# Seven products instead of eight for more row pairs of the MLP's up projection, with part of the preparation on GpSimd

## The chip, the cores and the metric

One core of one Trainium2 chip runs the kernel. The metric is the device time of one launch in microseconds (us); the time before is the median of three runs, and one further execution was recorded by the hardware profiler. Engines are called as the profile calls them: PE (TensorE), PEld (its weight loads), DVE (VectorE), ACT (ScalarE), POOL (GpSimd) and SP (SyncE, which issues most DMAs).

## What is computed

Two layers on 256 tokens of width 2048, all in float32. Layer 0 has a convolution module, layer 1 a latent attention; each is followed by the same kind of MLP, and the change touches only the two MLPs:

```python
def sq_relu_mlp(h, w1, w2):
    return jnp.square(jax.nn.relu(h @ w1)) @ w2

for layer in range(DEPTH):
    h = rms_norm(x, norm_mixer_g[layer])
    x = x + mixer(h)                       # conv_module or mla
    h = rms_norm(x, norm_mlp_g[layer])
    x = x + sq_relu_mlp(h, mlp_w1[layer], mlp_w2[layer])
```

Here `w1` is 2048 x 8192 and `w2` is 8192 x 2048.

## The kernel before

**Three products for one.** A float32 matrix is split into an upper part `hi` (rounded by ACT to the short float32 form that PE multiplies in one pass) and a lower part `lo` (what is left: a subtraction `raw - hi`). A product is then made of three matmuls, hi x hi, lo x hi and hi x lo (`mm3`, L209 to L211). Weights arrive by DMA in tiles `raw` of 128 x 2048 numbers (three buffers), ACT writes `hi`, DVE writes `lo`; there are six buffers of 128 x 1024 for each. So every weight passes ACT and DVE before PE can use it, and these engines run ahead of PE as far as the buffers allow.

**The MLP.** It is worked in two halves of 4096 hidden columns (`hf` 0 and 1). A half has an up projection, which makes eight groups of 512 hidden columns, and then a down projection, which adds the half's share to `x` in two pairs of 512-column blocks (`Sums`, L563; the very last pair of the program in two steps). `UP_PLAN` (L47) lists the order of the up projection. Four groups are made one at a time with the weights standing in PE and the input moving (L797 to L814). The other four are made as two *blocks* of two groups each (`up_block`, L732): here the input stands in PE and 512 columns of weights move at a time. Before, the plan is group 4, group 5, block 0 and 1, group 6, block 2 and 3, group 7.

**Eight products and seven.** In a block and in the down projection, the contraction is worked in *row pairs*: two stretches of 128 rows, for two sets of 128 tokens and two sets of 512 columns. That is a product of 2 x 2 matrices whose elements are blocks: eight products of three matmuls each (`Sums.plain`, L592: 24 matmuls). `Sums.mixed` (L579) does it with seven products (21 matmuls), by sums and differences of weight blocks on one side (`mixed_weights`, L517) and of input blocks on the other (`mixed_sums`, L539). The weights of such a pair need more work ahead of PE: four tiles of hi and lo instead of two (`b11` with `b21`; `b22`, half as large; `t1` with `t3`; `t4` with `t2`), and three subtractions on `raw` in place between them (L532 to L534). These depend on each other: `t1`, `t3` come from the first subtraction, `t4`, `t2` from the last. PE takes the products in the order b11, b21, b22, t1, t3, t4, t2 (L588).

A block has eight row pairs, in the order `UP_ORDER`; those in `UP_MIXED` go by seven products, before four of eight (2, 3, 4 and 5). Their input forms are made once in a half by `up_forms` (L680): a sum of hi and lo, four sums and differences, and a split, all three kinds on DVE, with the upper parts and copies on ACT. They stand in the buffers `s`. For the plain pairs of a block a copy of the input is made (`UP_COPIES`, `up_copies`). In the down projection seven or eight of the sixteen row pairs of a pair of column blocks go by seven products, mixed among plain ones; their input forms are made by `mixed_inputs` (L546) right after a group's squared ReLU.

**What sets the order.** The MLP's instructions are put in order by the framework's scheduler when the program is built, and each engine then runs its own list strictly in that order; an instruction that waits holds up all behind it on its engine. Buffers are handed out in rotation. GpSimd has little in the MLPs: it issues the DMAs that add finished sums to `x` (L611). It works in the convolution, where it makes lower parts of weights (L180 with `nc.gpsimd`), and in the attention, where it rotates keys and queries (L1529 to L1534).

Of the kernel before, what the change touches and what calls it, by code (L numbers as in the profile page):

```python
# [10 lines left out]
F32 = mybir.dt.float32  # L11
# [32 lines left out]
MIXED = {(layer, half): tuple(range(7 + (layer + half < 2))) for layer in range(2) for half in range(2)}  # L44
N_MIXED = 4
HEAD, TAIL = (2, 1), 2
UP_PLAN, UP_ORDER, UP_MIXED = (4, 5, 0, 6, 2, 7), (0, 2, 1, 3, 6, 4, 5, 7), (2, 3, 4, 5)  # L47
UP_FORMS = ({(1, 1): 0, (1, 3): 1}, {(0, 2): 0, (1, 1): 1})
UP_COPIES = ({(1, 0): 0, (1, 2): 3}, {(1, 0): 0, (1, 2): 3})


SIDE = {KC - 3: 2, KC - 2: 4}
# [30 lines left out]
def trunk_kernel(  # L83
# [59 lines left out]
    def nm(s):  # L143
        uid[0] += 1
        return f"{s}_{uid[0]}"
# [371 lines left out]
    def mixed_weights(raw):  # L517

        def halves(src):
            hi = wpool.tile(list(src.shape), F32R, tag="hi", name=nm("hi"), bufs=WB)
            lo = wpool.tile(list(src.shape), F32R, tag="lo", name=nm("lo"), bufs=WB)
            nc.scalar.activation(hi, src, AF.Copy)  # L524
            nc.vector.tensor_tensor(lo, src, hi.bitcast(F32), op=ALU.subtract)  # L525
# [6 lines left out]
        nc.vector.tensor_tensor(top, raw[:, :, NB:], top, op=ALU.subtract)  # L532
        nc.vector.tensor_tensor(low[:, 1, :], low[:, 1, :], top[:, 0, :], op=ALU.subtract)
        nc.vector.tensor_tensor(low[:, 0, :], low[:, 0, :], low[:, 1, :], op=ALU.subtract)  # L534
        t1, t3 = halves(top)
        t4, t2 = halves(low)
        return b11, b21, b22, t1, t2, t3, t4

    def mixed_sums(a11, a21, a12, a22):  # L539

        nc.vector.tensor_tensor(a22, a21, a22, op=ALU.add)
        nc.vector.tensor_tensor(a21, a11, a21, op=ALU.subtract)
        nc.vector.tensor_tensor(a11, a22, a11, op=ALU.subtract)
        nc.vector.tensor_tensor(a12, a12, a11, op=ALU.subtract)

    def mixed_inputs(v, fh, fl):  # L546

        def halves(src, at, n):  # L550
            hi, lo = fh[:, :, at : at + n, :], fl[:, :, at : at + n, :]
            nc.scalar.activation(hi, src, AF.Copy)
            nc.vector.tensor_tensor(lo, src, hi.bitcast(F32), op=ALU.subtract)
# [98 lines left out]
    def mlp(layer, ssq, next_gain, finish=None, before=None, beside=None, after_up=None):  # L652

        with ExitStack() as cx:
# [77 lines left out]
            def up_block(hf, g, fs, copies):  # L732

                n = (hf * nkh + 4 * g) // 4
                sums = Sums(n, False, True)
                left = [p for p in UP_ORDER if p in UP_MIXED]

                def at_kt(c):
                    def at(k, t):
                        ts = slice(t * P, (t + 1) * P)  # L740
                        return copies[k // 4][c][:, k % 4, ts] if k // 4 in copies else (xh, xl)[c](k)[:, ts]
                    return at

                for p in UP_ORDER:
                    if p in UP_MIXED:
                        left.remove(p)
                        sums.mixed(mlp_w1[layer], 2 * p, up_form(p, fs), not left)
                        continue
                    end = p == UP_ORDER[-1]
                    if end:  # L750
                        zs = [v_tile().rearrange("p k n -> p (k n)") for _ in range(T)]
                        sums.parts(*(z[:, c * NB : (c + 1) * NB] for z in zs for c in range(2)))
                    sums.plain(mlp_w1[layer], 2 * p, at_kt(0), at_kt(1), 2 * p, end)
                for t, z in enumerate(zs):
                    o = z.rearrange("p (c n) -> p c n", c=2)
                    nc.vector.tensor_tensor(o, sums.pairs[t], o, op=ALU.add)
                    nc.scalar.activation(z, z, AF.Relu, scale=r_cols[0][:, t : t + 1])

                def turned():
                    pts = [a.rearrange("p b (k t n) -> p (b k) t n", t=T, n=P) for a in sums.pairs]  # L760
                    for c in range(2):
                        for f in range(4):
                            for t in range(T):
                                at = c * NB + f * P
                                nc.tensor.transpose(pts[c][:, f, t, :], zs[t][:, at : at + P], ident)  # L765
                    for c in range(2):
                        place(g + c)
                        v = v_tile()
                        nc.scalar.activation(v, pts[c].rearrange("p f t n -> p f (t n)"), AF.Square)
                        activations(g + c, v)  # L770

                return [turned]

            r_cols, late = [], []
            for hf in range(HALVES):
# [5 lines left out]
                fs = [[mp.tile([P, 2, 7, P], F32R, tag=f"s{c}", name=nm(f"f{c}"), bufs=N_MIXED) for _ in range(2)] for c in "hl"]  # L781
                copied = {
                    n: [mp.tile([P, 4, S], F32R, tag=f"g{c}", name=nm(f"x{c}"), bufs=ng - N_MIXED) for c in "hl"]
                    for n in UP_COPIES[hf].values()
                }
                for nth, g in enumerate(UP_PLAN):
# [1303 lines left out]
```

## Time and profile before

| | |
|---|---|
| median of 3 runs | 1923.65 us (1923.41 to 1924.89) |
| the profiled execution | 1923.38 us, of which the span of the records is 1921.6 us |
| granted TensorE clock over the span | 0.999 |
| PE busy | 1909.4 us (99%) |
| DVE busy | 1696.6 us (88%) |
| ACT busy | 1201.3 us (63%) |
| POOL busy | 248.6 us (13%) |
| moved by DMA | 375.43 MB |

The convolution ends and layer 0's MLP begins at 301 us, the attention follows at about 977 us, and layer 1's MLP runs from about 1237 us to the end. A row of a timeline gives the start (us from the span's start), how long, the engine, the line, the operation, what is written from what, and the shape. Matmuls overlap: a matmul of 512 columns is shown as 0.39 us long, but the next starts before it ends, so PE's pace is read from start to start. In rows of the view that groups instructions, the numbers behind the bar are the group's busy time in us and the mean of one in ns.

### The profile page before, as it was taken

The page shows a single profiled execution, that of the slowest core. Times are in us where ns is not written, and L with a number is a line of the kernel's source. Part 1 is how long each engine was busy: PE and PEld are TensorE (multiplying, and loading weights), DVE is VectorE, ACT ScalarE, POOL GpSimd, SP SyncE. Part 2 cuts the span into 40 slices and gives each one's busy share as a digit, 9 for nine tenths or more (in the row PEclk, how much of TensorE's full clock was granted, in tenths as well). Part 3 has the DMA queues.
Part 4 walks back from the last instruction along what each step waited for, and adds up shares of the span by engine and source line. Part 5 has one row for each costly group of instructions (what it writes and reads, how often), then busy time and mean ns, then how long its engine had stood idle before and what let it go on. Part 6 is the DMA issues. An engine that isn't in the chain of part 4 may idle for free.

```text
span 1921.6 us, 27587 instructions
## 1 busy us (share of the span) xinstructions
PE 1909.4 (99%) x10245; PEld 1653.2 (86%) x10245; DVE 1696.6 (88%) x2407; ACT 1201.3 (63%) x1701; POOL 248.6 (13%) x208
## 2 busy tenths in 40 slices
PE   9999999999999999999999999999999999999998
PEld 9999888888888888888888998888888888888887
DVE  7999989999999899999976765898999988898898
ACT  5667756666655666665576665576665647666554
POOL 6999200000010100000001420000000010000000
PEclk9999999999999999999999999999999999999999
DMA  7766455556585855655656445556556775655774
GB/s 228 211 185 186 156 186 196 187 186 219 176 250 198 252 167 193 229 178 199 217 168 183 138 137 177 173 176 219 188 173 225 219 246 199 219 180 195 233 221 147
DMA packets 214039, 375.43 MB, mean 195 GB/s; under 512 B 16392, under 2 KB 107792, under 8 KB 213648
## 3 DMA queue, kind: packets, MB, share of 16 engines
q1 hardware_dynamic: 208256, 363.28, 57.4%
q0 software_dynamic: 4320, 7.87, 2.2%
q10 hardware_dynamic: 1328, 2.52, 0.4%
q8 instruction: 80, 1.31, 0.3%
q14 instruction: 55, 0.45, 0.1%
HBM read 363.68 MB, written 2.10 MB: 190 GB/s over the span
## 4 chain that ended last, share of the span: by engine, by line
PE 96%; DVE 2%; ACT 1%; issue 0%; DMA 0%; DVEq 0%; ACTq 0%
PE acc L209 11%; PE acc L211 11%; PE acc L210 11%; PE pair L211 10%; PE pair L210 10%; PE pair L209 10%; PE acc L812 9%; PE acc L972 8%; PE acc L813 5%; PE pair L812 3%; PE acc L1436 2%; PE pair L813 2%; DVE sum L1059 1%; PE pair L765 1%; PE acc L1713 0%
## 5 line engine op out<-in xcount | busy, mean ns | idle before, releaser
L176 ACT ACTIVATE hi<-raw 128x1024 fp32r<-128x1024 f32 (+2 forms) x510 | 509.9, 1030 | 149.1 <-DMA raw<-in_mlp_w 44.1
L180 DVE TENSOR_TENSOR lo<-raw,hi 128x1024 fp32r<-128x1024 f32 (+2 forms) x445 | 519.2, 1193 | 89.4 <-ACT hi L176 84.7
L524 ACT ACTIVATE hi<-raw 128x1024 fp32r<-128x1024 f32 x376 | 347.0, 948 | 316.0 <-DVE raw L532 199.1
L525 DVE TENSOR_TENSOR lo<-raw,hi 128x1024 fp32r<-128x1024 f32 x376 | 400.2, 1088 | 26.9 <-ACT hi L524 21.0
L812 PE MATMUL acc<-xt,hi 128*128 128x512 f32 x768 | 268.0, 391 | 0.0
L813 PE MATMUL acc<-xt,lo 128*128 128x256 f32 x768 | 216.5, 282 | 0.0
L972 PE MATMUL acc<-xt,hi 128*128 128x256 f32 x1024 | 180.2, 281 | 0.4 <-ACT xt L1239 0.3
L611 POOL DMA_DIRECT2D xs<-v x30 | 26.3, 932 | 1128.3 <-DVE lo L180 696.2
L812 PEld LDWEIGHTS acc<-xt,hi 128*128 128x128 f32 x768 | 144.2, 188 | 30.1
L1059 DVE SCALAR_TENSOR_TENSOR sum<-ub,w_dw,sum 128x256 f32<-128x256 f32 x409 | 164.4, 485 | 3.6 <-ACT sum L1029 3.0
L180 POOL TENSOR_TENSOR lo<-raw,hi 128x1024 fp32r<-128x1024 f32 x65 | 155.0, 2408 | 18.0 <-ACT hi L176 18.0
L972 PEld LDWEIGHTS acc<-xt,hi 128*128 128x128 f32 x1024 | 154.7, 188 | 1.2 <-ACT xt L1239 0.8
L813 PEld LDWEIGHTS acc<-xt,lo 128*128 128x128 f32 x768 | 145.1, 189 | 0.3
L972 PE MATMUL acc<-xt,lo 128*128 128x256 f32 x512 | 139.2, 279 | 0.0
L532 DVE TENSOR_TENSOR raw<-raw 128x1024 f32<-128x1024 f32 x94 | 114.8, 1221 | 0.4
L209 PE MATMUL acc<-hi,sh 128*128 128x512 f32 x289 | 112.6, 390 | 0.0
L211 PE MATMUL acc<-lo,sh 128*128 128x512 f32 x289 | 112.5, 389 | 0.0
L210 PE MATMUL pair<-hi,gl 128*128 128x512 f32 (+1 forms) x264 | 101.9, 386 | 0.0
L211 PE MATMUL pair<-lo,gh 128*128 128x512 f32 (+1 forms) x264 | 101.9, 386 | 0.0
L209 PE MATMUL pair<-hi,gh 128*128 128x512 f32 (+1 forms) x264 | 101.9, 386 | 0.0
L209 PE MATMUL acc<-hi,gh 128*128 128x512 f32 x252 | 98.1, 389 | 0.0
L211 PE MATMUL acc<-lo,gh 128*128 128x512 f32 x252 | 98.0, 389 | 0.0
(381 smaller groups left out, 4299.1 us busy)
## 6 DMA issues: line engine op xcount, KB each, us to landing
raw<-in_mlp_w SPq DMA_DIRECT2D x255, 1024.0 KB, 5.5
raw<-in_conv_w_pw SPq DMA_DIRECT2D x62, 512.0 KB, 5.1
raw<-in_conv_w_pw SPq DMA_DIRECT2D x16, 1024.0 KB, 4.9
raw<-in_mla_w_o SPq DMA_DIRECT2D x16, 1024.0 KB, 5.1
raw<-in_mla_w_kv_up SPq DMA_DIRECT2D x32, 256.0 KB, 4.0
xs<-v POOLq DMA_DIRECT2D x30, 256.0 KB, 7.3
raw<-in_mla_w_in SPq DMA_DIRECT2D x8, 576.0 KB, 4.3
raw<-in_mla_w_in SPq DMA_DIRECT2D x4, 1024.0 KB
```

Of the source, the lines that this page charges most:

```text
L176: nc.scalar.activation(hi, raw[:, js, :], AF.Copy)
L180: eng.tensor_tensor(lo, raw, hi.bitcast(F32), op=ALU.subtract)
L209: nc.tensor.matmul(ps, sh, mh, start=start, stop=False)
L210: nc.tensor.matmul(ps, sl, mh, start=False, stop=False)
L211: nc.tensor.matmul(ps, sh, ml, start=False, stop=stop)
L524: nc.scalar.activation(hi, src, AF.Copy)
L525: nc.vector.tensor_tensor(lo, src, hi.bitcast(F32), op=ALU.subtract)
L532: nc.vector.tensor_tensor(top, raw[:, :, NB:], top, op=ALU.subtract)
L812: nc.tensor.matmul(ps[b], wh[:, bs], xhl(k), start=k == 0, stop=False)
L813: nc.tensor.matmul(ps[b][:, :S], wl[:, bs], xh(k), start=False, stop=k == KC - 1)
L972: nc.tensor.matmul(pss[c][b][:, :S], w[i][:, bs], (xh, xl)[j](k), start=k == i + j == 0, stop=end and k == k0 + nk - 1 and (i, j) == terms ...
L1059: nc.vector.scalar_tensor_tensor(out=out, in0=ubs[c][:, w : w + S], scalar=tap(c, w), in1=base, op0=ALU.mult, op1=ALU.add)
```

## The change

More row pairs of the blocks go by seven products: six of eight (`UP_MIXED` is 0 to 5), in the order 6, 0, 1, 2, 3, 4, 5, 7, so that the six stand side by side. The plan of the up projection becomes group 4, group 5, block 6 and 7, group 0, block 1 and 2, group 3 (`UP_BLOCKS` says which places of the plan are blocks, since a block may now consist of groups that the down projection takes by eight products). Three input forms are made instead of two, and one input tile is copied instead of two; form tiles and copies share the buffers `s`. And some work moves from DVE to GpSimd: the lower parts of `b22` and of `t1` with `t3` in every mixed row pair, the blocks' and the down projection's; everything that `up_forms` does on DVE; and the last lower part of `mixed_inputs`. What is computed is the same.

```diff
-UP_PLAN, UP_ORDER, UP_MIXED = (4, 5, 0, 6, 2, 7), (0, 2, 1, 3, 6, 4, 5, 7), (2, 3, 4, 5)
-UP_FORMS = ({(1, 1): 0, (1, 3): 1}, {(0, 2): 0, (1, 1): 1})
-UP_COPIES = ({(1, 0): 0, (1, 2): 3}, {(1, 0): 0, (1, 2): 3})
+UP_PLAN, UP_BLOCKS, UP_ORDER, UP_MIXED = (4, 5, 6, 0, 1, 3), (2, 4), (6, 0, 1, 2, 3, 4, 5, 7), (0, 1, 2, 3, 4, 5)
+UP_FORMS = ({(1, 0): 0, (1, 1): 1, (1, 2): 2}, {(0, 2): 0, (1, 0): 1, (1, 1): 2})
+UP_COPIES = ({(1, 0): 3}, {(1, 0): 3})
...
-        def halves(src):
+        def halves(src, eng=nc.vector):
...
-            nc.vector.tensor_tensor(lo, src, hi.bitcast(F32), op=ALU.subtract)
+            eng.tensor_tensor(lo, src, hi.bitcast(F32), op=ALU.subtract)
...
-        (b22,) = halves(raw[:, 1:2, NB:])
+        (b22,) = halves(raw[:, 1:2, NB:], nc.gpsimd)
...
         nc.vector.tensor_tensor(top, raw[:, :, NB:], top, op=ALU.subtract)
+        t1, t3 = halves(top, nc.gpsimd)
         nc.vector.tensor_tensor(low[:, 1, :], low[:, 1, :], top[:, 0, :], op=ALU.subtract)
         nc.vector.tensor_tensor(low[:, 0, :], low[:, 0, :], low[:, 1, :], op=ALU.subtract)
-        t1, t3 = halves(top)
         t4, t2 = halves(low)
...
-    def mixed_sums(a11, a21, a12, a22):
+    def mixed_sums(eng, a11, a21, a12, a22):
...
-        mixed_sums(*(v[:, :, i, :] for i in range(4)))
-        halves(v, 3, 4)
+        mixed_sums(nc.vector, *(v[:, :, i, :] for i in range(4)))
+        halves(v, 3, 4, nc.gpsimd)
...
-                nc.vector.tensor_tensor(v, x[:, :, :S], x[:, :, S:], op=ALU.add)
+                nc.gpsimd.tensor_tensor(v, x[:, :, :S], x[:, :, S:], op=ALU.add)
...
-                mixed_sums(*(v[:, :, j, :] for j in range(4)))
+                mixed_sums(nc.gpsimd, *(v[:, :, j, :] for j in range(4)))
...
-                nc.vector.tensor_tensor(l, v, h.bitcast(F32), op=ALU.subtract)
+                nc.gpsimd.tensor_tensor(l, v, h.bitcast(F32), op=ALU.subtract)
...
-                    if g in mixed:
-                        late = up_block(hf, g, fs, {n: a for n, a in copied.items() if nth < 3 or n > 0})
+                    if nth in UP_BLOCKS:
+                        late = up_block(hf, g, fs, copied if nth == UP_BLOCKS[0] else {})
```

PE's list has 10198 matmuls before and 10150 after, 48 fewer: three for each of two more row pairs in eight blocks.

**DVE in a block.** Before, in the second block of layer 0's first half, these are DVE's rows for the last two mixed row pairs, which stand next to each other (`raw_666` and `raw_675`; numbers behind names tell tiles apart):

```order
L525 TENSOR_TENSOR lo_668_4995<-raw_666_4992,hi_667_4994 128x1024
L525 TENSOR_TENSOR lo_670_4999<-raw_666_4992,hi_669_4998 128x512
L532 TENSOR_TENSOR raw_666_4992<-raw_666_4992 128x1024
L533 TENSOR_TENSOR raw_666_4992<-raw_666_4992 128x512
L534 TENSOR_TENSOR raw_666_4992<-raw_666_4992 128x512
L525 TENSOR_TENSOR lo_672_5006<-raw_666_4992,hi_671_5005 128x1024
L525 TENSOR_TENSOR lo_674_5010<-raw_666_4992,hi_673_5009 128x1024
L525 TENSOR_TENSOR lo_677_5037<-raw_675_5034,hi_676_5036 128x1024
```

After, at the same block, the third and fourth of the six mixed row pairs (`raw_665` and `raw_674`; the lines have moved by one, so that L534 and L535 are what L533 and L534 were):

```order
L525 TENSOR_TENSOR lo_667_4945<-raw_665_4942,hi_666_4944 128x1024
L532 TENSOR_TENSOR raw_665_4942<-raw_665_4942 128x1024
L534 TENSOR_TENSOR raw_665_4942<-raw_665_4942 128x512
L535 TENSOR_TENSOR raw_665_4942<-raw_665_4942 128x512
L525 TENSOR_TENSOR lo_673_4960<-raw_665_4942,hi_672_4959 128x1024
L525 TENSOR_TENSOR lo_676_4987<-raw_674_4984,hi_675_4986 128x1024
```

Seven rows for one row pair have become five; nothing stands any more between the last subtraction (L534 before, L535 after) and the lower part that is made of its result.

**GpSimd there.** Before, its list has only the DMAs of L611 in this MLP; after, these rows stand there for the same two row pairs and the one ahead of them (`sl_634` is the last lower part of group 0's input forms):

```order
L525 TENSOR_TENSOR lo_660_4907<-raw_656_4900,hi_659_4906 128x512
L525 TENSOR_TENSOR lo_662_4912<-raw_656_4900,hi_661_4911 128x1024
L553 TENSOR_TENSOR sl_634_4796<-v_635_4797,sh_633_4795 128x2x512
L525 TENSOR_TENSOR lo_669_4949<-raw_665_4942,hi_668_4948 128x512
L525 TENSOR_TENSOR lo_671_4954<-raw_665_4942,hi_670_4953 128x1024
L525 TENSOR_TENSOR lo_678_4991<-raw_674_4984,hi_677_4990 128x512
```

Two rows for each row pair, and one for a form, have come to GpSimd's list.

**ACT ahead of the first block.** Before, in the same half, ACT's rows around the upper part of the second (last) input form, `fh_463` (`hi_524` and `hi_537` are upper parts of weights of group 5 and of the block's first, plain row pair):

```order
L176 ACTIVATE hi_524_4182<-raw_521_4176 128x1024
L691 ACTIVATE fh_463_3801<-xt_3_98 128x2x128
L692 ACTIVATE fh_463_3801<-xt_3_98 128x2x256
L687 ACTIVATE fh_463_3801<-v_526_4218 128x2x512
L691 ACTIVATE fl_465_3803<-xt_3_98 128x2x128
L692 ACTIVATE fl_465_3803<-xt_3_98 128x2x256
L176 ACTIVATE hi_537_4253<-raw_536_4251 128x1024
```

After, around that of the third (last) form, `fh_466`:

```order
L692 ACTIVATE fl_469_3807<-xt_3_98 128x2x256
L176 ACTIVATE hi_524_4200<-raw_523_4198 128x1024
L687 ACTIVATE fh_466_3804<-v_522_4186 128x2x512
L176 ACTIVATE hi_526_4204<-raw_523_4198 128x1024
L176 ACTIVATE hi_538_4263<-raw_537_4261 128x1024
```

The form's upper part now stands ahead of group 5's last weights (`hi_526`), and it waits for GpSimd's sums.

More of the change, by code (lines that the diff above doesn't have):

```diff
@@ L532, in mixed_weights, with halves @@
         nc.vector.tensor_tensor(top, raw[:, :, NB:], top, op=ALU.subtract)
+        t1, t3 = halves(top, nc.gpsimd)
         nc.vector.tensor_tensor(low[:, 1, :], low[:, 1, :], top[:, 0, :], op=ALU.subtract)
         nc.vector.tensor_tensor(low[:, 0, :], low[:, 0, :], low[:, 1, :], op=ALU.subtract)
-        t1, t3 = halves(top)
         t4, t2 = halves(low)
         return b11, b21, b22, t1, t2, t3, t4
-    def mixed_sums(a11, a21, a12, a22):
[L541 to L544, printed above, removed]
+    def mixed_sums(eng, a11, a21, a12, a22):
+        eng.tensor_tensor(a22, a21, a22, op=ALU.add)
+        eng.tensor_tensor(a21, a11, a21, op=ALU.subtract)
+        eng.tensor_tensor(a11, a22, a11, op=ALU.subtract)
+        eng.tensor_tensor(a12, a12, a11, op=ALU.subtract)
     def mixed_inputs(v, fh, fl):
-        def halves(src, at, n):
+        def halves(src, at, n, eng=nc.vector):
             hi, lo = fh[:, :, at : at + n, :], fl[:, :, at : at + n, :]
             nc.scalar.activation(hi, src, AF.Copy)
-            nc.vector.tensor_tensor(lo, src, hi.bitcast(F32), op=ALU.subtract)
+            eng.tensor_tensor(lo, src, hi.bitcast(F32), op=ALU.subtract)
         halves(v[:, :, 0:1, :], 0, 1)
         halves(v[:, :, 2:4, :], 1, 2)
-        mixed_sums(*(v[:, :, i, :] for i in range(4)))
-        halves(v, 3, 4)
+        mixed_sums(nc.vector, *(v[:, :, i, :] for i in range(4)))
+        halves(v, 3, 4, nc.gpsimd)
     def by_pairs(v):
@@ L780, in mlp @@
                 gs = {}
-                fs = [[mp.tile([P, 2, 7, P], F32R, tag=f"s{c}", name=nm(f"f{c}"), bufs=N_MIXED) for _ in range(2)] for c in "hl"]
                 copied = {
-                    n: [mp.tile([P, 4, S], F32R, tag=f"g{c}", name=nm(f"x{c}"), bufs=ng - N_MIXED) for c in "hl"]
+                    n: [mp.tile([P, 4, S], F32R, tag=f"s{c}", name=nm(f"x{c}"), bufs=N_MIXED) for c in "hl"]
                     for n in UP_COPIES[hf].values()
                 }
+                fs = [
+                    [mp.tile([P, 2, 7, P], F32R, tag=f"s{c}", name=nm(f"f{c}"), bufs=N_MIXED) for _ in range(len(UP_MIXED) // 2)]
+                    for c in "hl"
+                ]
                 for nth, g in enumerate(UP_PLAN):
-                    if g in mixed:
-                        late = up_block(hf, g, fs, {n: a for n, a in copied.items() if nth < 3 or n > 0})
+                    if nth in UP_BLOCKS:
+                        late = up_block(hf, g, fs, copied if nth == UP_BLOCKS[0] else {})
                         continue
```

## Prediction

> **What bounds the kernel now.** First the page's busy times and its chain that ended last, then the waits of PE:
>
> ```profile
> PE 1909.4 (99%) x10245; PEld 1653.2 (86%) x10245; DVE 1696.6 (88%) x2407; ACT 1201.3 (63%) x1701; POOL 248.6 (13%) x208
> ...
> PE 96%; DVE 2%; ACT 1%; issue 0%; DMA 0%; DVEq 0%; ACTq 0%
> ```
> ```profile
> PE acc L1150 <- POOL ident masks.py:199: 1.6, 1, 1.6
> PE acc L209 <- DVE xt L222: 1.2, 1, 1.2
> ```
>
> PE bounds it: it waits 1.6 us once and 1.2 us once, and never for weights in an MLP. So matmuls left out are gained in full as long as the weights still come in time. What one is worth is read from start to start; PE's timeline over a mixed row pair of a block, from its first matmul over the second to the first of what follows:
>
> ```profile
> 441.24 0.39 PE L209 MATMUL acc<-hi,fh 128*128 128x512 f32 x1
> 441.46 0.39 PE L210 MATMUL acc<-hi,fl 128*128 128x512 f32 x1
> ...
> 446.00 0.39 PE L209 MATMUL pair<-hi,xh 128*128 128x512 f32 x1
> ```
>
> The 21 matmuls take 446.00 - 441.24 = 4.76 us, 0.2267 us each, not the 0.39 us of a record. A plain row pair's 24 take 5.44 us.
>
> The other side of a block is the preparation. The grouped view, each shape by itself:
>
> ```profile
> L525 DVE TENSOR_TENSOR lo<-raw,hi 128x1024 fp32r<-128x1024 f32 x282 | 341.7, 1222 | 26.9 <-ACT hi L524 21.0
> L532 DVE TENSOR_TENSOR raw<-raw 128x1024 f32<-128x1024 f32 x94 | 114.8, 1221 | 0.4
> L533 DVE TENSOR_TENSOR raw<-raw 128x512 f32<-128x512 f32 x94 | 65.1, 692 | 3.0
> L534 DVE TENSOR_TENSOR raw<-raw 128x512 f32<-128x512 f32 x94 | 65.0, 692 | 2.6
> L525 DVE TENSOR_TENSOR lo<-raw,hi 128x512 fp32r<-128x512 f32 x94 | 64.5, 686 | 0.0
> L524 ACT ACTIVATE hi<-raw 128x1024 fp32r<-128x1024 f32 x282 | 295.4, 1057 | 296.4 <-DVE raw L532 199.1 <-DVE raw L534 40.4 <-PE pair L210 13.8
> ```
>
> DVE needs 3 x 1.22 + 1.22 + 2 x 0.69 + 0.69 = 6.95 us for a mixed row pair that PE finishes in 4.76, and 2 x 1.22 = 2.4 us for a plain one that PE takes 5.44 us for. A mixed pair overdraws the lead, a plain one pays back. How large the lead is when a block's mixed pairs begin: DVE's first lower part for the first one, and PE's first matmul on it:
>
> ```profile
> 340.92 1.22 DVE L525 TENSOR_TENSOR lo<-raw,hi 128x1024 fp32r<-128x1024 f32 x1
> ```
> ```profile
> 351.00 0.39 PE L209 MATMUL acc<-hi,fh 128*128 128x512 f32 x1
> ```
>
> 10.1 us; the rotation of six buffers lets it hardly grow.
>
> **What goes.** 48 matmuls of 0.2267 us: 10.9 us off PE, if it never waits. On paper DVE is relieved too: 6.95 - 1.22 - 0.69 = 5.04 us per mixed pair, nearly PE's 4.76.
>
> **What the mixed pair costs now.** Two things speak against those 5.04 us. The first is a gap. ACT and DVE around the last subtractions of a pair:
>
> ```profile
> 440.18 1.06 ACT L524 ACTIVATE hi<-raw 128x1024 fp32r<-128x1024 f32 x1 [2.78 <-DVE raw L532]
> 441.63 1.06 ACT L524 ACTIVATE hi<-raw 128x1024 fp32r<-128x1024 f32 x1 [0.39 <-DVE raw L534]
> ```
> ```profile
> 440.82 0.69 DVE L534 TENSOR_TENSOR raw<-raw 128x512 f32<-128x512 f32 x1
> 441.43 2.51 DVE L525 TENSOR_TENSOR lo<-raw,hi 128x1024 fp32r<-128x1024 f32 x2
> ```
>
> The last subtraction ends at 441.51; ACT rounds its result from 441.63 to 442.69; only then can DVE make that lower part. Before, DVE fills the time with the other lower part. After, its list has nothing in between, and the next pair's rows stand behind: 1.2 us idle, 6.2 us per pair.
>
> The second is GpSimd beside DVE. GpSimd's own prices, from the views by line and by shape:
>
> ```profile
> L180 POOL TENSOR_TENSOR lo<-raw,hi x65: 2352/2409/2445, 12.7 to 197.9; 128x1024 fp32r<-128x1024 f32 x65
> ```
> ```profile
> L1748 POOL TENSOR_TENSOR qhl<-qp,qhl 128x256 fp32r<-128x256 f32 x8 | 5.8, 734 | 0.9 <-ACT qhl L215 0.9
> ```
>
> (2409 - 734) / 768 = 2.18 ns per element, so 2.41 us for 1024 columns and an estimate of 1.29 us for 512. The 2409 hold beside a DVE that in the convolution reads one operand from PSUM. In an MLP both operands of lower parts and subtractions lie in SBUF. The only place of the trace where DVE does such work while GpSimd subtracts or adds is the attention; GpSimd's timeline, then DVE's, and last DVE's two lower parts in the MLP with GpSimd idle:
>
> ```profile
> 1045.71 0.45 POOL L1531 TENSOR_TENSOR m<-scratch,cos 128x128 f32<-128x128 f32 x1
> 1046.13 1.44 POOL L1532 TENSOR_TENSOR m<-scratch,sin 128x128 f32<-128x128 f32 x1
> ...
> 1086.60 0.46 POOL L1532 TENSOR_TENSOR m<-scratch,sin 128x128 f32<-128x128 f32 x1
> 1087.02 1.49 POOL L1533 TENSOR_TENSOR qp<-m,m 128x128 f32<-128x128 f32 x1
> ```
> ```profile
> 1045.71 2.94 DVE L180 TENSOR_TENSOR lo<-raw,hi 128x1024 fp32r<-128x1024 f32 x2 [1.71 <-ACT hi L176]
> ...
> 1086.96 1.23 DVE L180 TENSOR_TENSOR lo<-raw,hi 128x1024 fp32r<-128x1024 f32 x1 [0.32 <-ACT hi L176]
> ```
> ```profile
> 444.15 2.36 DVE L180 TENSOR_TENSOR lo<-raw,hi 128x1024 fp32r<-128x1024 f32 x2 [0.20 <-PE acc L211]
> ```
>
> A GpSimd operation of 0.46 us takes 1.49 us when a DVE lower part has begun 0.06 us earlier: it ends 0.32 us after that one. And DVE loses in turn: the two lower parts from 1045.71 take 2.94 us instead of 2.36, with the two GpSimd operations of 1045.71 and 1046.13 fitted in, 0.29 us each, which is 128 x 2.18 ns. The two engines take turns. GpSimd thus costs DVE 1024 x 2.18 = 2.2 us and 512 x 2.18 = 1.1 us for a mixed pair: 5.04 + 2.2 + 1.1 = 8.3 us, with the gap hidden under GpSimd's turn. ACT's four upper parts, at most 4 x 1.06 us, stay below that, and the DMAs carry what they did before.
>
> The Trainium skill says in "SBUF — State Buffer", section "Who interferes with whom", that a VectorE instruction with two SBUF inputs contends with a GpSimd instruction that reads SBUF, and that the pair of ports is held exclusively for the whole instruction. By its whole instruction DVE would lose 2.41 + 1.29 = 3.7 us, 8.7 us per pair, and the sum below would be 35 us more; the attention's rows show turns, but only 0.29 us of a 0.46 us operation. I take the row.
>
> Ends for the hold: nothing (6.2 us per pair, as the convolution's rows would have it) and the whole operation (5.04 + 2.41 + 1.29 = 8.7 us). The attention's rows are the same operations on the same operands, so 8.3.
>
> **A block.** Six pairs stand side by side, so PE wants them in 6 x 4.76 = 28.6 us. Preparation begins 10.1 us ahead and takes six times C, and with it the evacuation of the group before, which DVE's list has among the first pairs; that and other work of the blocks:
>
> ```profile
> L832 DVE SCALAR_TENSOR_TENSOR v<-v,r_row 128x1024 f32<-128x1024 f32 x16 | 19.6, 1224 | 0.1
> L715 DVE TENSOR_TENSOR gl<-v,gh 128x1024 fp32r<-128x1024 f32 x16 | 19.5, 1221 | 2.1 <-ACT gh L714 2.1
> L541 DVE TENSOR_TENSOR v<-v 128x256 f32<-128x256 f32 x23 | 9.6, 419 | 0.1
> L553 DVE TENSOR_TENSOR sl<-v,sh 128x512 fp32r<-128x512 f32 x16 | 11.0, 689 | 0.8
> L1486 DVE SCALAR_TENSOR_TENSOR v<-v 128x64 f32<-128x64 f32 x19 | 4.3, 225 | 0.3
> ```
>
> That is 2.4 us (L832, L715). GpSimd's long lower part is ready about 1.1 us before a pair's preparation ends, and PE, which meets it as the twelfth matmul, then needs 2.3 us to end the pair: +1.2. PE's wait in a block is 6 C - 10.1 + 2.4 + 1.2 - 28.6 = 6 C - 35.1: 14.7 us for 8.3, 2.1 for 6.2, 17.1 for 8.7, none below 5.85. Eight blocks: 118 us.
>
> More is in some. The second block of a half follows group 0, which has mixed input forms: four sums of 0.42, lower parts of 0.69 and (256 columns like L541) 0.42 and GpSimd's 2.2 us, 5 us, four times: 20. In layer 0's second half some 28 small operations of the rotary tables (0.225 us, L1486) fall into the end of group 5 and the first block: 5 of their 6 us. In the first halves three forms go one behind the other through GpSimd, each 2 x 2.41 + 4 x 0.73 + ACT's 1.06 = 8.8 us, the last two behind group 4's evacuation; group 5, during which they must end, lasts from the first to the second of these rows:
>
> ```profile
> 323.36 0.39 PE L812 MATMUL acc<-xt,hi 128*128 128x512 f32 x1
> ...
> 345.54 0.39 PE L209 MATMUL pair<-hi,xh 128*128 128x512 f32 x1
> ```
>
> 17.6 of 22.2 us, and the third form's upper part stands on ACT ahead of the last eighth of group 5's weights, which PE wants 2.8 us before that end, and of all the block's. Estimate: 10 us of wait and lost lead, between 0 and 14, twice: 20. Blocks in all 163 us.
>
> **The down projection.** Eight pairs of column blocks, each about eight mixed and eight plain row pairs: 8 x (8.3 + 2.4) = 85.6 us of preparation against 8 x (4.76 + 5.44) = 81.6 of PE, 4 us more even if leads carried over everything. Where two mixed pairs and a plain one follow each other, 19.0 stand against 15.0, three times in the first pair of columns: 12. I take 8, 64 us in all (32 to 96). Fewer input sums on DVE, copies and group order change nothing that PE waits for: group 3's forms come last and are used last.
>
> **Sum**, on the profiled execution's 1923.4 us (its span and 1.8 us around; the median of the runs is 0.3 us above): - 10.9 + 163 + 64 = + 216, **2140 us**.
>
> **Rivals.**
> - *The turns don't matter at this size, only the gap does* (6.2): for it, the convolution's 2409; against, the attention's rows. Blocks 8 x 2.1 + 45, columns none (14.8 against 15.0): + 62 - 10.9, 1975 us. Chance 0.08.
> - *All is hidden, faster*: GpSimd's work falls into DVE's gaps and the lead bears the rest; decides below 5.85 us per pair. For it, DVE's 5.04; against, both rows above. 1912.5 us. Chance 0.05.
> - *PE's clock falls in the waits*: with 8.3 us per pair PE stands still for 3.5 us each time. At half the clock a pair would take 9.5 us and bound itself: 48 x 1.2 = 58 us more, 2198 us. The trace grants full speed, but has no such wait. Chance 0.05. (The Trainium skill, "TensorE: Matmul & The Clock Gate", Part 1, halves the clock after an idle window of about 3.4 us; no run here shows it.)
>
> The forecast has 0.82. With a hold of two thirds (C 7.2: blocks 8 x 8.1 + 20, no columns) it would be 1997; with the whole hold, 14 us twice and 12 per columns, 2198. Range 1990 to 2210, with which the gap alone and the gain stay out. Faster by over 0.2% (about what can be told from no change) 0.05, within 0.01, slower 0.94.
>
> **What would show it.** In the profile after, PE waits for POOL `lo` L525, and DVE's records of L525 and L532 grow past 1.22 us or POOL's past 2.41, in blocks and in the down projection; from one mixed pair's first lower part to the next 8.3 us; a block's matmuls last some 39.4 + 14.7 = 54 us instead of 4 x (4.76 + 5.44) = 41. Wrong is the turn if POOL shows 2.41 and DVE 1.22 side by side; wrong is all of it if PE has no wait in the blocks.

## The result and the profile after

The changed kernel takes 2223.9 us (median of four runs, 2221.7 to 2224.1) against 1923.6 before: 1.156 times as long, with an interval of 1.1537 to 1.1577. The forecast was 2140 us with a range up to 2210. The direction and, in the blocks' row pairs, the mechanism were right; the size was 84 us too small, 51 of them in the down projections. The profiled execution took 2223.85 us, its span is 2222.1 us.

The page's busy times:

```profile
PE 2027.1 (91%) x10197; PEld 1678.5 (76%) x10197; DVE 1806.2 (81%) x2203; ACT 1227.7 (55%) x1745; POOL 893.6 (40%) x516
```

PE has 48 matmuls less in its list, yet it is busy for 118 us more, and DVE, which was to be relieved, for 110 us more. Then the waits of PE (us in all, how often, the longest):

```profile
PE acc L211 <- POOL lo L525: 67.4, 45, 2.0
PE pair L211 <- POOL lo L525: 33.8, 20, 2.6
PE acc L209 <- ACT hi L524: 19.6, 23, 1.7
PE acc L815 <- ACT hi L176: 11.7, 6, 3.4
```

PE waited for nothing in an MLP before. Now it waits 101 us for GpSimd's lower parts (the first two rows) and another 31 us for upper parts, which are late because DVE's subtractions are (L524) or because ACT is held up (L176). The grouped view of DVE and GpSimd says what made them late:

```profile
L525 DVE TENSOR_TENSOR lo<-raw,hi 128x1024 fp32r<-128x1024 f32 x220 | 408.3, 1873 | 130.8 <-ACT hi L524 128.0 <-PE acc L210 1.2 <-PE pair L211 1.2
L532 DVE TENSOR_TENSOR raw<-raw 128x1024 f32<-128x1024 f32 x110 | 174.8, 1589 | 3.5
```
```profile
L525 POOL TENSOR_TENSOR lo<-raw,hi 128x1024 fp32r<-128x1024 f32 x110 | 277.8, 2525 | 302.8 <-ACT hi L524 187.7 <-PE pair L211 50.0 <-issue 42.5
L525 POOL TENSOR_TENSOR lo<-raw,hi 128x512 fp32r<-128x512 f32 x110 | 207.9, 1890 | 334.0 <-ACT hi L524 295.9 <-PE acc L211 17.7 <-PE pair L210 13.2
...
L553 POOL TENSOR_TENSOR sl<-v,sh 128x512 fp32r<-128x512 f32 x1 | 1.3, 1273 | 6.1 <-ACT sh L552 6.1
```

DVE's lower part was 1222 ns and its long subtraction 1221; they are 1873 and 1589. GpSimd's short lower part was estimated at 1.29 us, and the one of 512 columns outside the row pairs (L553) took 1.27; in the row pairs it shows 1.89. And in front of these lower parts of DVE stands idle time that ACT ends, once in a mixed pair: 128 us in all, about 1.2 us for each of the 110 pairs.

Where in the program this falls, from the windows view of layer 0's first half; columns: the window, its length, the busy time of PE, PEld, DVE, ACT and POOL, the granted clock, the DMA share and GB/s. The rows are groups 4 and 5, the first block, the second block, the down projection; first before:

```profile
300.92:345.54 44.62, 44.62 (x259) 39.55 (x258) 41.39 (x64) 33.13 (x48) 0.00 (x0) 1.00 0.52 177
345.54:386.36 40.82, 40.82 (x183) 33.79 (x182) 37.65 (x41) 26.30 (x32) 0.00 (x0) 1.00 0.55 189
410.31:451.44 41.13, 41.13 (x183) 33.80 (x182) 39.65 (x44) 26.78 (x33) 0.00 (x0) 1.00 0.53 181
475.40:638.62 163.22, 163.22 (x723) 135.19 (x722) 152.25 (x161) 94.32 (x108) 8.31 (x10) 1.00 0.67 212
```
```profile
300.70:355.20 54.50, 47.90 (x259) 41.31 (x258) 36.64 (x48) 32.35 (x47) 21.81 (x14) 0.94 0.38 128
355.20:414.36 59.16, 47.23 (x179) 33.90 (x178) 49.05 (x43) 31.01 (x38) 23.64 (x11) 0.94 0.39 134
437.85:498.34 60.49, 47.87 (x178) 34.99 (x177) 49.83 (x45) 30.41 (x37) 25.93 (x12) 0.92 0.35 117
521.84:713.74 191.90, 176.12 (x722) 138.20 (x721) 160.64 (x133) 95.47 (x111) 87.65 (x45) 0.96 0.56 180
```

The granted clock is a second new thing: 1.00 in each of these stages before, 0.92 to 0.96 now. Summed over the four halves, from the start of PE's first matmul in each stage, and beside it what the prediction had for the same stages (118 + 20 + 5 - 10.9 = 132 for the blocks):

| stage, four halves | before | after | forecast | measured |
|---|---|---|---|---|
| groups 4 and 5 | 178.0 | 216.2 | +20 | +38 |
| the eight blocks | 327.9 | 479.1 | +132 | +151 |
| the other two groups | 191.7 | 188.0 | 0 | -4 |
| down projections | 651.8 | 767.1 | +64 | +115 |

Last a steady stretch of a block, the fourth and fifth of the six mixed pairs; DVE's timeline, then GpSimd's:

```profile
379.30 4.33 DVE L525 TENSOR_TENSOR lo<-raw,hi 128x1024 fp32r<-128x1024 f32 x2 [1.21 <-ACT hi L524]
383.66 1.23 DVE L532 TENSOR_TENSOR raw<-raw 128x1024 f32<-128x1024 f32 x1
384.99 0.69 DVE L534 TENSOR_TENSOR raw<-raw 128x512 f32<-128x512 f32 x1
385.72 0.69 DVE L535 TENSOR_TENSOR raw<-raw 128x512 f32<-128x512 f32 x1
387.62 4.31 DVE L525 TENSOR_TENSOR lo<-raw,hi 128x1024 fp32r<-128x1024 f32 x2 [1.21 <-ACT hi L524]
391.96 1.23 DVE L532 TENSOR_TENSOR raw<-raw 128x1024 f32<-128x1024 f32 x1
```
```profile
377.81 2.51 POOL L525 TENSOR_TENSOR lo<-raw,hi 128x1024 fp32r<-128x1024 f32 x1 [2.31 <-ACT hi L524]
380.87 1.68 POOL L525 TENSOR_TENSOR lo<-raw,hi 128x512 fp32r<-128x512 f32 x1 [0.55 <-ACT hi L524]
```

From L532 to L532 a pair takes 391.96 - 383.66 = 8.30 us; 8.3 was forecast. It is made up of 5.14 us of DVE's own work, the gap of 1.21 us, and 4.31 - 2.36 = 1.95 us by which the two lower parts are longer. The gap before the lower parts at 379.30 lasts from 378.09 to 379.30 and lies wholly within GpSimd's long instruction, 377.81 to 380.32. The ends of the records show how DVE loses them. GpSimd's second instruction ends at 380.87 + 1.68 = 382.55 and DVE's second lower part at 379.30 + 4.33 = 383.63, 1.08 us later; alone that lower part needs 1.22. So all but 0.14 us of its work came behind the end of GpSimd's instruction.

### The profile page after: what moved, and what is told of

Same layout as the page of the kernel before. It is cut to its first block, busy times and chain, and to the rows that moved or that the text cites. A ratio compares the mean times of both kernels' runs of the same rounds, so it can differ in the third digit from the quotient of the medians.

```text
span 2222.1 us, 27868 instructions
## 1 busy us (share of the span) xinstructions
PE 2027.1 (91%) x10197; PEld 1678.5 (76%) x10197; DVE 1806.2 (81%) x2203; ACT 1227.7 (55%) x1745; POOL 893.6 (40%) x516
## 5 line engine op out<-in xcount | busy, mean ns | idle before, releaser
L525 POOL TENSOR_TENSOR lo<-raw,hi 128x512 fp32r<-128x512 f32 x220 | 485.3, 2208 | 636.8 <-ACT hi L524 483.6
L524 ACT ACTIVATE hi<-raw 128x1024 fp32r<-128x1024 f32 (+1 forms) x440 | 402.8, 946 | 501.5 <-DVE raw L532 329.3
L180 DVE TENSOR_TENSOR lo<-raw,hi 128x1024 fp32r<-128x1024 f32 (+2 forms) x413 | 502.5, 1247 | 137.6 <-ACT hi L176 131.5
L176 ACT ACTIVATE hi<-raw 128x1024 fp32r<-128x1024 f32 (+2 forms) x478 | 472.6, 1027 | 148.0 <-DMA raw<-in_mlp_w 69.9
L525 DVE TENSOR_TENSOR lo<-raw,hi 128x1024 fp32r<-128x1024 f32 x220 | 408.3, 1873 | 130.8 <-ACT hi L524 128.0
L532 DVE TENSOR_TENSOR raw<-raw 128x1024 f32<-128x1024 f32 x110 | 174.8, 1589 | 3.5
L211 PE MATMUL acc<-lo,fh 128*128 128x512 f32 x192 | 87.3, 470 | 57.2 <-POOL lo L525 53.6
L534 DVE TENSOR_TENSOR raw<-raw 128x512 f32<-128x512 f32 x110 | 104.3, 948 | 35.2 <-POOL lo L525 25.1
L211 PE MATMUL pair<-lo,sh 128*128 128x512 f32 x225 | 96.2, 427 | 26.2 <-POOL lo L525 23.1
L553 POOL TENSOR_TENSOR sl<-v,sh 128x1024 fp32r<-128x1024 f32 (+1 forms) x16 | 48.5, 3043 | 166.9 <-ACT sh L552 166.9
L209 PE MATMUL pair<-hi,sh 128*128 128x512 f32 x225 | 93.7, 417 | 17.1 <-ACT v L647 6.6
```

The lines of the kernel that those rows point to most:

```text
L176: nc.scalar.activation(hi, raw[:, js, :], AF.Copy)
L180: eng.tensor_tensor(lo, raw, hi.bitcast(F32), op=ALU.subtract)
L209: nc.tensor.matmul(ps, sh, mh, start=start, stop=False)
L211: nc.tensor.matmul(ps, sh, ml, start=False, stop=stop)
L525: eng.tensor_tensor(lo, src, hi.bitcast(F32), op=ALU.subtract)
```

## The experiments

All times are medians; "changed" is the changed kernel, 2223.9 us. Lines in these kernels can lie up to five off those of the changed one; `...` in a diff stands for lines left out.

**1. All on DVE.** GpSimd's new work goes back; six mixed pairs and order stay.

```diff
-        (b22,) = halves(raw[:, 1:2, NB:], nc.gpsimd)
+        (b22,) = halves(raw[:, 1:2, NB:])
-        t1, t3 = halves(top, nc.gpsimd)
...
+        t1, t3 = halves(top)
         t4, t2 = halves(low)
...
```

> The changed kernel with all of GpSimd's new work back on DVE: six mixed pairs side by side and the new group order stay. My theory (GpSimd's share is what costs, about 8.3 us per mixed pair against 7.0 on DVE alone): a mixed pair comes every 7.0 us, the wait in a block falls to about 6 x 7.0 - 36.3 = 5.7 us, the down projection takes the 163 us per half that it took before, group 5 loses at most the 4 us of a third input form; with 48 matmuls less, 1923 - 11 + 46 + 4 x 3 for the second blocks + 8 = about 1980 us, with a granted clock near 1. Rival (the six mixed pairs side by side and the new order cost the time, whoever makes the lower parts): over 2150 us.

Measured: 1994.7 us, clock 0.996, 1.037 times before (1.035 to 1.0391). DVE over one pair in a block, with four lower parts in the second row:

```profile
367.93 1.22 DVE L532 TENSOR_TENSOR raw<-raw 128x1024 f32<-128x1024 f32 x1
...
370.51 4.25 DVE L525 TENSOR_TENSOR lo<-raw,hi 128x1024 fp32r<-128x1024 f32 x4
374.69 1.22 DVE L532 TENSOR_TENSOR raw<-raw 128x1024 f32<-128x1024 f32 x1
```

6.76 us per pair, no gap, every record at its price of before. So 229 of the 300 us are GpSimd's share, and 71 are the six pairs and the order: +56 in the blocks, 48 matmuls less included, and +17 in the down projections. Groups 4 and 5 take what they took before (178.0 us), with three forms on DVE instead of two.

**2. The other lower part to GpSimd.** DVE fills its gap with `t1`, `t3`; GpSimd makes `t4`, `t2`.

```diff
-        t1, t3 = halves(top, nc.gpsimd)
...
-        t4, t2 = halves(low)
+        t1, t3 = halves(top)
+        t4, t2 = halves(low, nc.gpsimd)
```

> The changed kernel, but DVE makes the lower part of t1 with t3 behind the last subtraction, as before the change, and GpSimd that of t4 with t2 instead. Nothing is idle then on DVE while ACT rounds the last subtraction's result. If the gap of 1.2 us is an addend of the 8.3 us and the time that GpSimd holds DVE stays 2.0 us: 7.1 us per mixed pair, 58 us less in the blocks and some 25 in the down projection, about 2140 us. If GpSimd shuts DVE out for its whole instruction and only the gap had taken part of that off the path: 5.04 + 2.4 + 1.3 = 8.7 us per mixed pair, between 2210 and 2250 us, with DVE records of L525 of 2.3 us and hardly any idle DVE.

Measured: 2236.6 us. The time is in the second case's range, but the gap has not gone: DVE is idle again, in front of the next pair's first lower part. Its rows, then GpSimd's:

```profile
892.06 2.20 DVE L532 TENSOR_TENSOR raw<-raw 128x1024 f32<-128x1024 f32 x1
...
897.93 2.56 DVE L525 TENSOR_TENSOR lo<-raw,hi 128x1024 fp32r<-128x1024 f32 x1 [1.02 <-ACT hi L524]
```
```profile
897.03 4.61 POOL L525 TENSOR_TENSOR lo<-raw,hi 128x1024 fp32r<-128x1024 f32 x2 [3.85 <-ACT hi L524]
```

The gap has moved by one lower part, since ACT rounds the next pair's weights only behind `t4`, `t2`. With a gap and a hold of 1.34 + 0.98 us by these two records a pair takes 8.46 us. As in the changed kernel, nearly all of the gap lies beside a GpSimd instruction, the one that begins at 897.03. So the run has no pair without a gap, and does not tell the two cases apart.

**3. GpSimd's lower parts left out** (upper parts stand in for them).

```diff
-            lo = wpool.tile(list(src.shape), F32R, tag="lo", name=nm("lo"), bufs=WB)
+            lo = wpool.tile(list(src.shape), F32R, tag="lo", name=nm("lo"), bufs=WB) if eng is nc.vector else hi
...
-            eng.tensor_tensor(lo, src, hi.bitcast(F32), op=ALU.subtract)
+            if eng is nc.vector:
+                eng.tensor_tensor(lo, src, hi.bitcast(F32), op=ALU.subtract)
```

> The changed kernel with GpSimd's lower parts of b22, t1 and t3 left out: their upper parts stand in for them as operands, so PE does as many matmuls and DVE keeps its gap, but GpSimd reads nothing there. What is left out of the computation is the lower halves of these products. GpSimd keeps the input forms. If the two hold each other up: a mixed pair every 6.2 to 6.3 us, DVE's records of L525 back at 1.22 us, waits of 2 to 3 us per block; 1923 - 11 + 8 x 2 + 20 for the second blocks + 38 for group 5 + some 10 per down projection for the input form on GpSimd = about 2020 us. If DVE's gap and its own chain set the pace and not GpSimd: no less than 2150 us.

Measured: 2014.1 us. DVE's order is that of the changed kernel, gap included:

```profile
374.87 1.22 DVE L533 TENSOR_TENSOR raw<-raw 128x1024 f32<-128x1024 f32 x1
...
378.83 2.36 DVE L526 TENSOR_TENSOR lo<-raw,hi 128x1024 fp32r<-128x1024 f32 x2 [1.21 <-ACT hi L524]
381.22 1.23 DVE L533 TENSOR_TENSOR raw<-raw 128x1024 f32<-128x1024 f32 x1
```

6.35 us per pair instead of 8.30. Without GpSimd reading, 1.95 us go, and 2223.9 - 2014.1 = 210 us of the whole; 110 mixed pairs by 1.95 are 215.

**4. Matmuls against the clock.** Eight matmuls with a zero tile fill PE's wait in each mixed pair of a block.

```diff
+    zeros = const.tile([P, 64], F32R, name="zeros")
+    nc.scalar.activation(zeros, ident[:, :64], AF.Copy, scale=0.0)
...
-            for ps, i, (wh, wl) in work:
+            for nth, (ps, i, (wh, wl)) in enumerate(work):
...
+                if self.up and nth == 2:
+                    for _ in range(8):
+                        nc.tensor.matmul(ps[:64, :], zeros, wh, start=False, stop=False)
```

> The changed kernel with eight more matmuls in every mixed pair of a block, ahead of t1 where PE waits for GpSimd: a stationary tile of zeros, so they add nothing to the sums. 384 matmuls more, 87 us of PE's time at full speed. If the half-speed matmuls behind a wait cost time of their own (about 29 of 0.43 us in each block): the granted clock in the blocks goes from 0.91 to 0.94 to nearly 1, and the whole falls by 20 to 40 us, to 2185 to 2205 us. If preparation alone sets the pace of the blocks, and the clock falls only where PE has time: within 8 us of 2224. If the added matmuls are not hidden in the waits: 2240 us or more.

Measured: 2212.7 us over four runs (2210.0 to 2214.6), between the first two cases. The window of a second block:

```profile
436.76:494.26 57.50, 53.03 (x225) 38.60 (x224) 46.96 (x42) 29.04 (x36) 25.24 (x12) 1.00 0.37 125
```

The clock is 1.00, and 384 more matmuls made the kernel 11 us faster; the blocks together take 15 us less. So the slower clock costs something, but DVE's pace in the steady pairs (8.34 us here) leaves PE time for most of it.

**5. The blocks' input forms on DVE** (`up_forms`: three lines back to `nc.vector`).

```diff
...
-                mixed_sums(nc.gpsimd, *(v[:, :, j, :] for j in range(4)))
+                mixed_sums(nc.vector, *(v[:, :, j, :] for j in range(4)))
...
```

> The changed kernel with only the blocks' input forms back on DVE; GpSimd keeps the weights' lower parts and the last lower part of the down projection's inputs. My theory: the time that group 4 and 5 lost in all four halves (9.2 to 9.9 us each, 38 in all) is the chain of forms on GpSimd and goes, while blocks and down projection stay: 2224 - 38 = 2186 us. The prediction's own account (only the first halves pay, 10 us each): 2204 us. Rival (the blocks take the lead that group 5 gains and the sum hardly moves): over 2210 us.

Measured: 2189.4 us; groups 4 and 5 are back at 44.6 and 44.4 us in all halves. The forms on GpSimd cost 34.5 us, in second halves as much as in first ones.

**6. The last lower part of `mixed_inputs` on DVE.**

```diff
-        halves(v, 3, 4, nc.gpsimd)
+        halves(v, 3, 4)
```

> The changed kernel with only the last lower part of the down projection's input forms (L553, 1024 columns) back on DVE. My theory: group 3's stands on GpSimd ahead of the lower parts of the second mixed pair's weights and costs some 5 to 8 us at the start of each down projection, with the slower clock behind it: 20 to 30 us less, about 2198 us. Rival (DVE is late there anyway, and the lower part costs the same on it): within 6 us of 2224.

Measured: 2202.0 us, 22 less: 16 in the down projections, 7 in the blocks.

**7. and 8. GpSimd for the weights of the blocks alone, and of the down projections alone** (`if not up` in the line below); everything else on DVE.

```diff
+        eng = nc.gpsimd if up else nc.vector
...
-        (b22,) = halves(raw[:, 1:2, NB:], nc.gpsimd)
+        (b22,) = halves(raw[:, 1:2, NB:], eng)
...
```

> Only the blocks' weights have their lower parts of b22, t1 and t3 on GpSimd; those of the down projection, the forms and the inputs are on DVE (the first experiment with this added). If the terms add up: each block goes from 48 to about 60 us, eight blocks, 1995 + 8 x 12 = 2091 us, down projections unchanged. If GpSimd's costs share a wait with the forms: below 2070.

> Only the down projection's weights have their lower parts of b22, t1 and t3 on GpSimd; the blocks, the forms and the inputs are on DVE. The prediction's own account of the steady state (8 us per pair of column blocks): 1995 + 64 = 2059 us. If GpSimd's share of the weights makes the whole of what the down projections lost: 1995 + 100 = 2095 us. If a third of the loss is the input forms' lower part on GpSimd, and not the weights: about 2070 us.

Measured: 2084.8 us and 2074.3 us. Against the first experiment that is 90 us for the blocks and 80 for the down projections, the latter nearest to the third case. The shares add up:

| share of the 300 us | runs | us |
|---|---|---|
| six pairs and order, on DVE | 1 - before | 71.6 |
| blocks' weights on GpSimd | 7 - 1 | 90.1 |
| down projections' weights on GpSimd | 8 - 1 | 79.6 |
| blocks' input forms on GpSimd | changed - 5 | 34.5 |
| down projections' inputs on GpSimd | changed - 6 | 21.9 |
| sum | | 297.7 |

**9. The smallest share.** The first experiment, with `b22`'s lower part alone on GpSimd; the edit is against the changed kernel.

```diff
         (b22,) = halves(raw[:, 1:2, NB:], nc.gpsimd)
...
-        t1, t3 = halves(top, nc.gpsimd)
...
+        t1, t3 = halves(top)
...
-        halves(v, 3, 4, nc.gpsimd)
+        halves(v, 3, 4)
...
```

> The first experiment with the smallest share on GpSimd: only the lower part of b22, 512 columns, in every mixed row pair. DVE is spared 0.69 us per pair, GpSimd's instruction takes 1.28 us. If GpSimd shuts DVE out for its whole instruction: a mixed pair every 6.76 - 0.69 + 1.28 = 7.35 us, 0.6 more than with DVE alone, 8 x 6 x 0.6 = 28 us in the blocks and some 15 in the down projections, about 2038 us. If a small share fits between DVE's instructions: 6.1 to 6.3 us per pair, below 1980 us.

Measured: 2052.3 us. A pair takes 7.32 us. GpSimd's instruction and DVE's beside it:

```profile
896.85 2.00 POOL L525 TENSOR_TENSOR lo<-raw,hi 128x512 fp32r<-128x512 f32 x1 [5.33 <-ACT hi L524]
```
```profile
894.04 3.65 DVE L525 TENSOR_TENSOR lo<-raw,hi 128x1024 fp32r<-128x1024 f32 x3
897.73 2.19 DVE L532 TENSOR_TENSOR raw<-raw 128x1024 f32<-128x1024 f32 x1
900.03 0.69 DVE L533 TENSOR_TENSOR raw<-raw 128x512 f32<-128x512 f32 x1
```

GpSimd ends at 898.85, DVE at 899.92, 1.07 us later, as in the changed kernel. From start to start the subtraction takes 900.03 - 897.73 = 2.30 us instead of 1.25, and the lower parts ahead of it 3.69 instead of 4.18: DVE loses 1.05 and is spared 0.49. Even this share costs 57.6 us in all, 29 in the blocks where 28 were expected and 26 instead of 15 in the down projections.

**10. GpSimd in the kernel before.** Its order and its four mixed pairs per block, only the weights' lower parts moved.

```diff
...
-        (b22,) = halves(raw[:, 1:2, NB:])
+        (b22,) = halves(raw[:, 1:2, NB:], nc.gpsimd)
...
+        t1, t3 = halves(top, nc.gpsimd)
...
-        t1, t3 = halves(top)
...
```

> The kernel before, with its four mixed row pairs in a block and its order, and only the lower parts of b22, t1 and t3 moved to GpSimd. If GpSimd's share is what costs, whatever the order: the down projections lose the same 80 us as with the new order, and a block, with 4 x 8.3 + 4 x 2.4 + 2.4 = 45 us of preparation against 40.8 of matmuls, some 2 to 6 us: 1923 + 80 + 16 to 48, about 2035 us. If it costs only where mixed pairs stand side by side: below 1990 us.

Measured: 2053.8 us, +130: 78 in the down projections, as with the new order, and 47 in the blocks, the upper end of what was expected. It doesn't need six pairs side by side.

**11. GpSimd writing without reading.** Two fills with zeros for each of its lower parts (the lower halves are zero then).

```diff
-                eng.tensor_tensor(lo, src, hi.bitcast(F32), op=ALU.subtract)
+            if eng is nc.vector:
+                eng.tensor_tensor(lo, src, hi.bitcast(F32), op=ALU.subtract)
+            for _ in range(2 * (eng is nc.gpsimd)):
+                eng.memset(lo.bitcast(F32), 0.0)
```

> The changed kernel with each of GpSimd's lower parts of b22, t1 and t3 replaced by two fills of the same tile with zeros: GpSimd writes as much, twice over, and reads nothing. The lower halves of these products are left out of the computation. Two fills of 1024 columns are estimated at 2.1 us from the trace's 0.31 us for 256, so GpSimd is about as long busy per pair as before. If GpSimd shuts DVE out by reading beside it: a mixed pair every 6.35 us as in the third experiment, DVE's records of L525 back at 1.22 us, 2010 to 2035 us. If GpSimd's mere activity or its writing into the same memory does it: DVE's records stay near 1.9 us and the time is over 2150 us.

Measured: 2016.6 us, 6.35 us per pair. The groups of GpSimd, then of DVE:

```profile
L528 POOL MEMSET lo<- 128x1024 f32 x220 | 210.4, 956 | 59.4 <-PE pair L211 33.6 <-PE acc L819 14.3 <-PE acc L211 6.5
L528 POOL MEMSET lo<- 128x512 f32 x220 | 119.0, 541 | 511.9 <-PE pair L211 190.8 <-PE acc L211 182.7 <-PE acc L819 133.5
```
```profile
L526 DVE TENSOR_TENSOR lo<-raw,hi 128x1024 fp32r<-128x1024 f32 x220 | 269.8, 1243 | 138.1 <-ACT hi L524 134.7 <-PE acc L210 1.2 <-PE pair L210 1.2
```

GpSimd is busy for 329 us with fills and DVE's lower part takes 1243 ns. Some 175 of DVE's lower parts and subtractions of 1024 columns run beside a fill, at a median of 1224 ns; the twelve that take over 1.4 us all meet a lower part of an input form of the down projection, which GpSimd still subtracts there. It is GpSimd's reading beside DVE that holds DVE up, not its writing and not its being at work. The Trainium skill says just that in "SBUF — State Buffer", section "Who interferes with whom": a VectorE instruction with two SBUF inputs contends with a GpSimd instruction that reads SBUF and not with one that only writes it.

No version points below the kernel before: on DVE alone six pairs ask 6.76 us where PE asks 4.76, and every share of a pair's lower parts that was tried on GpSimd made the pair longer (7.32, 8.30 and 8.46 us).

## Why the prediction was too low

- **The pair's 8.3 us** came out (8.30), and so did its parts within 0.15 us: 5.14 us of DVE's own work for 5.04, and 1.21 + 1.95 = 3.16 us of gap and longer records for the 3.3 us that GpSimd was to take, "with the gap hidden under GpSimd's turn". Of the 2.51 us of the long instruction (377.81), 1.49 pass before DVE begins its lower part, and the gap is inside them. Experiment 3 shows what is left without GpSimd's reading: with the gap, 6.35 us. That a pair without a gap would gain nothing beside GpSimd is argued from these rows; no run shows it. The prediction's reason needs one correction. The rule that it set against its row, a hold for the whole instruction (the Trainium skill, "SBUF — State Buffer", section "SBUF: two separate sides"), agrees with these records but for 0.14 us: DVE ends 1.08 us after GpSimd, its full 1.22 less 0.14. The attention's own row does too: GpSimd's operation of 1046.13 ends at 1047.57, and DVE's two lower parts at 1048.65. But a hold costs only what of it falls into DVE's work, not the 3.7 us that the prediction put to it. Its price for that case is also given twice, as 35 us more and as 2198 us, which is 58 more.
- **The blocks** were 132 against 151: one of 54 us and one of 59 forecast, 59.2 and 60.5 measured. The steady pairs kept to 8.3 us; the first three of the first block, among which group 5's evacuation lies, took 383.66 - 354.82 = 28.8 us by the starts of their first subtractions (the row of 383.66 stands above):

```profile
354.82 1.23 DVE L532 TENSOR_TENSOR raw<-raw 128x1024 f32<-128x1024 f32 x1
```

  The evacuation was counted at 2.4 us, which leaves 1.5 us beyond three times 8.3. Experiment 4 puts about 15 us of the eight blocks on the slower clock.
- **The input forms** were 20 against 38. The mechanism was right: the third form's upper part holds up ACT, and with it the weights of group 5 and of the block; ACT's row for it, behind which stand the weights' upper parts:

```profile
345.73 1.06 ACT L687 ACTIVATE fh<-v 128x1024 fp32r<-128x1024 f32 x1 [5.01 <-POOL v L544]
346.69 1.99 ACT L176 ACTIVATE hi<-raw 128x1024 fp32r<-128x1024 f32 x2
```

  But the prediction counted it only in the first halves, 10 us "twice". The second halves start their forms one step earlier and lose 9.2 us each all the same, against 9.9 in the first.
- **The down projection is the step that failed**: 64 forecast, 96 at most, 115 measured. The steady row pairs were right; a mixed and a plain one, 8.3 + 2.4 = 10.7 us forecast, take 583.63 - 573.00 = 10.63:

```profile
573.00 0.69 DVE L534 TENSOR_TENSOR raw<-raw 128x512 f32<-128x512 f32 x1
...
583.63 0.69 DVE L534 TENSOR_TENSOR raw<-raw 128x512 f32<-128x512 f32 x1
```

  "I take 8" per pair of column blocks was 10 (80 us by experiment 8). And "copies and group order change nothing that PE waits for: group 3's forms come last and are used last" was wrong. They are used last, but they stand first: their last lower part lies on GpSimd ahead of the second mixed pair's weights. GpSimd, DVE and PE at the start of a down projection:

```profile
538.71 2.38 POOL L553 TENSOR_TENSOR sl<-v,sh 128x1024 fp32r<-128x1024 f32 x1 [7.25 <-ACT sh L552]
541.02 3.59 POOL L525 TENSOR_TENSOR lo<-raw,hi 128x512 fp32r<-128x512 f32 x2
```
```profile
542.34 2.83 DVE L534 TENSOR_TENSOR raw<-raw 128x512 f32<-128x512 f32 x1 [3.67 <-POOL lo L525]
```
```profile
544.67 0.80 PE L211 MATMUL acc<-lo,sh 128*128 128x512 f32 x1 [1.11 <-POOL lo L525]
...
552.38 0.63 PE L211 MATMUL pair<-lo,gh 128*128 128x512 f32 x1
```

  The weights' two lower parts (541.02) begin when the form's ends, DVE stands still for 3.67 us and then needs 2.83 for 0.69 us of work, and PE works at half pace up to 553 us. L534 overwrites in place numbers that `b22`'s lower part reads, so it has to wait for GpSimd. Experiment 6, which moves this lower part and that of the other groups' forms back, puts 16 us of the down projections on them, experiment 1 another 17 on the order.
- **The rivals.** The clock did fall, which had 0.05 and 58 us; it cost far less, about 15 us in the blocks, since a block's pace is DVE's. What it costs outside the blocks was not isolated. "Only the gap" is what experiments 3 and 11 stage: 2014 and 2017 us. 1975 was forecast for it, with 20 us for the forms, which took 41 there, 31 for the rest of the blocks, which took 43, and nothing for the order in the down projections, which took 12.

Why the new order costs 17 us in the down projections even on DVE alone stays open; group 3's input forms, which lie directly ahead of them there too, are the nearest cause, but no run took them alone. In layer 0's first half of experiment 1, PE falls 3.2 us behind the kernel before over the 720 matmuls of the down projection, 2.4 of them in the first 150.

## What to carry to other kernels

In this kernel GpSimd was no spare VectorE for elementwise work with all operands in SBUF. While it subtracted or added there, a VectorE subtraction of two SBUF operands stood still but for 0.14 us, and GpSimd took 1.27 us for 512 columns that VectorE does in 0.69. Before work is moved there, look for a row of the trace in which both run on such operands, and compare when they end. And follow a moved instruction's place in the new engine's list: used last doesn't mean queued last.

## What the runs showed of the hardware

- A VectorE subtraction of 1024 columns that meets a GpSimd one ends 1.08 us after it (1.22 us alone), in each of 168 such meetings of L525 and L532 with GpSimd's L525 in the changed kernel; one of 512 columns ends 0.55 us after it (0.69 alone). Fills by GpSimd (956 ns for 1024 columns) leave the long one at 1.24.
- One wait of 2.4 us was enough to halve PE's pace, from about 0.6 us after it and for 3.4 us: PE's timeline in a down projection, behind the wait and at the end of the slow stretch:

```profile
627.63 0.50 PE L209 MATMUL pair<-hi,sh 128*128 128x512 f32 x1 [2.40 <-ACT v L647]
...
628.20 0.59 PE L211 MATMUL pair<-lo,sh 128*128 128x512 f32 x1
628.59 0.63 PE L209 MATMUL acc<-hi,sh 128*128 128x512 f32 x1
629.02 0.63 PE L210 MATMUL acc<-hi,sl 128*128 128x512 f32 x1
...
631.58 0.43 PE L210 MATMUL pair<-hi,sl 128*128 128x512 f32 x1
631.85 0.39 PE L211 MATMUL pair<-lo,sh 128*128 128x512 f32 x1
```

  Starts lie 0.43 us apart instead of 0.23. The granted clock is 0.50 from 628.24 to 631.65 us, and PE was busy for 1.01 of the 3.41 us before. The Trainium skill, "TensorE: Matmul & The Clock Gate", Part 1, has windows of about 3.4 us, of which an idle one halves the clock; the length of the slow stretch agrees, but here the wait was shorter than a window.
